# Eighty elementwise operations of the MLPs and of the dilated v projection, taken from VectorE to GpSimd

## The chip, the cores and the metric

The kernel runs on one core of a Trainium2 chip. The metric is device time in microseconds (us) of one execution. TensorE is called PE below, VectorE DVE, ScalarE ACT, GpSimd POOL and SyncE SP, as in the profile.

## The reference

Two layers of an encoder trunk on one sequence of 1024 tokens with 1024 channels. Each layer has a token mixer (layer 0: latent attention with 16 heads; layer 1: three groups of dilated windowed attention) and a squared-ReLU MLP with 4096 hidden channels. Each half normalises its input, shifts and scales it by numbers that come from a conditioning vector (`mods`), and adds its result, times a gate, to the residual. All is float32.

```
for i in range(DEPTH):
    h = rms_norm(x, g) * (1 + scale) + shift
    x = x + gate * mixer(h)          # i=0: mla, i=1: dilated
    h = rms_norm(x, g) * (1 + scale) + shift
    x = x + gate * (square(relu(h @ mlp_w1[i])) @ mlp_w2[i])
```

The v projection of the dilated mixer is, for each of its three groups, a product of h (1024 by 1024) with a weight of 1024 by 1024.

## The kernel before, in words

A float32 product is made of three products in a form that PE takes in one pass: each operand is split into a high part (ACT copies it, L121) and a low part (DVE subtracts the high part from the operand, L122), and `mm3` (L425 to L427) multiplies high with high, low with high, high with low. So every tile of a weight or an activation that reaches PE has one ACT operation and one DVE operation ahead of it: in the MLP the tiles are `dh` and `dl` (made of `ufr`, `w2r`, `w2T`, `w2s`), in the v projection `wvh` and `wvl` (weights, made of `wvr`), `hT`, `hsh` and `hsl` (activations, made of `hk` and of the sums `s`).

The MLP (`mlp7`) and the v projection (`dil_v`) both replace eight block products by seven, in the manner of Strassen and Winograd: quarters of the operands are first added and subtracted, seven products are made, and their results are put together when PSUM is read out.

`mlp7` has an up phase, whose results (`ua`, `ub`, `us`) are stored to DRAM by POOL, and a down phase of seven products with eight steps each. A step is 24 matmuls of 128x512. Step by step the operands are loaded three steps ahead (`d_load`: `ufr` are the stored activations, `w2r` the weights) and formed one step ahead (`d_form`). Of the weights' quarters, product 0 (R11) loads quarters 11 and 12, splits 11 and at once subtracts 11 from 12; that difference and 11 are kept (16 tiles). Product 1 (T2) loads quarter 22, subtracts the kept difference (`w2T`, kept as well), splits that, and at once subtracts the kept 11 from it, in place; this is what product 5 (T3) uses. Product 2 (T1) uses the kept difference, and product 6 (T4) loads quarter 21, subtracts `w2T` (giving `w2s`) and splits the result. When a product is complete, `evict` reads PSUM; in products 3, 4 and 5 it ends with `fin`: z = z times the gate, x = x + z, on tiles of 128x512, and a store of x. The eviction of product 5 runs `fin` twice for each of four tiles (16 operations) and lies in the steps of product 6. In layer 0 those steps also hold the start of the next layer: the first half of its normalised input is transposed on PE (`pst`), shifted on ACT (`hk`) and split (`hT`), and the first weights of the v projection are split (`wvh`, `wvl`).

`dil_v` has 21 products of 48 matmuls, seven for each group, numbered n below. `sums` makes the weight sums of a group, eight subtractions of 128x1024: two in the first product of the group, four in the second, two in the third. The helper `sub` pins them to the order of the program. `h_sums` makes the sums of the activations (`s`, `hk`) on DVE. `out` evicts to a tile `vz` and has POOL store it. All through these stages DVE also adds the conditioning of later layers (`adacc`, L176), 128x1024 at a time.

A scheduler that works before the run puts the instructions of each engine in an order; on the chip each engine runs its own in that order and waits on semaphores.

Of the kernel before, what the change touches and what calls it, by code (L numbers as in the profile page):

```python
# [15 lines left out]
ALU = mybir.AluOpType  # L16
# [25 lines left out]
class K:  # L42
# [1045 lines left out]
    def mlp7(self, l, early, R, steps, xd, out, more=(), nxt=None, keep=None):  # L1088
# [7 lines left out]
        nc, a = self.nc, self.a  # L1096
        NP = FF // 256
        tt = lambda o, x, y, op=ALU.add: nc.vector.tensor_tensor(o, x, y, op=op)
# [6 lines left out]
        with self.tc.tile_pool(name="psM", bufs=8, space=PSUM, reuse_waits="tile") as psp:  # L1105
# [71 lines left out]
            kept = {}  # L1177
# [9 lines left out]
            def d_form(i, g, ld):  # L1187
                rn = order2[i][1]
                u, q = ld
                r = []  # L1190

                def split(x):
                    r.extend(self.X("d" + k, (P, 2, 512)) for k in "hl")
                    self.split(*r[-2:], x)

                split(u)
                if rn == "R11":
                    split(q["11"])
                    tt(q["12"], q["12"], q["11"], ALU.subtract)
                    kept[("T1", g)], kept[("T3", g)] = q["12"], q["11"]  # L1200
                elif rn == "T2":
                    kept[(rn, g)] = w = self.G("w2T", (P, 2, 512), F32)
                    tt(w, q["22"], kept[("T1", g)], ALU.subtract)
                    split(w)
                    tt(kept[("T3", g)], w, kept[("T3", g)], ALU.subtract)
                elif rn == "T4":
                    w = self.X("w2s", (P, 2, 512), F32)
                    tt(w, q["21"], kept[("T2", g)], ALU.subtract)
                    split(w)
                else:  # L1210
                    split(q[rn[1:]] if rn[0] == "R" else kept[(rn, g)])
                return r
# [16 lines left out]
            at = {ci: n for n, ci in enumerate(seq)}  # L1229
# [22 lines left out]
            def d_first(k, made):  # L1252
                if made:
                    fm[k] = d_form(*dsteps[k], ld.pop(k))
                else:
                    ld[k] = d_load(*dsteps[k])
# [37 lines left out]
            at = lambda q, t: q[t // 2][:, t % 2, :]  # L1294
            xs = [None] * 8
            last = len(dsteps) - 1
            c1, c2 = slice(0, 512), slice(512, 1024)
            V, done = {}, []

            def fin(t, c, y):  # L1300

                z = self.T("z")
                tt(z, y, g[:, c], ALU.mult)
                tt(xs[t][:, c], xs[t][:, c], z)

            def evict(i, t, ps):

                add = lambda o, v: tt(o, ps, at(V[v], t))
                new = {0: "S1", 1: "U2", 2: "U4", 5: "U3"}.get(i)
                if new and t == 0:  # L1310
                    V[new] = quad("d" + new)
                if i == 0:
                    nc.scalar.activation(at(V["S1"], t), ps, AF.Copy)
                    return
                if new:
                    add(at(V[new], t), {1: "S1", 2: "U2", 5: "U2"}[i])
                if i > 2:
                    z = self.T("z")
                    add(z, {3: "S1", 4: "U4", 5: "U4"}[i])
                    r, c = {3: (t, c1), 4: (t, c2), 5: (t + 4, c2)}[i]  # L1320
                    fin(r, c, z)
                    out(r, c, xs[r], nc.gpsimd)
                if i == 5:
                    fin(t + 4, c1, at(V["U3"], t))

            more = list(more)
            h = None
            for n, (i, gr) in enumerate(dsteps):
# [4 lines left out]
                for k in {0: (), last - 2: (last - 1, last), last - 1: (), last: ()}.get(n, (n + 1,)):  # L1333
                    fm[k] = d_form(*dsteps[k], ld.pop(k))
                if done:
                    evict(*done.pop(0))
                if gr == 0:
                    ps = [M() for _ in range(4)]
                if i in (3, 5) and gr < 4:
                    t = i * 2 - 6 + gr  # L1340
                    xs[t] = self.load(xd[t * P : (t + 1) * P, :], (P, 1024), "x")
                if (i, gr) == (3, 4):
                    g = self.gate(l, 1)
# [7 lines left out]
                for t in range(4):  # L1351
                    if n == last:
                        down(ps[t], fm[n - 1], t, False, False)
                    down(ps[t], fm[n], t, gr == 0, gr == NP // 2 - 1)
                    if n == last:
                        fin(t + 4, c1, ps[t])
                        out(t + 4, c1, xs[t + 4], nc.sync)
# [232 lines left out]
    def dil_v(self, xs, mods, at0, keep, w11, f11, vd):  # L1590
# [2 lines left out]

        nc, a = self.nc, self.a
        tt = lambda o, x, y, op=ALU.add: nc.vector.tensor_tensor(o, x, y, op=op)
        sub = lambda o, x, y: self.pinned(tt(o, x, y, ALU.subtract))

        prod = [("L11", "R11"), ("L12", "R21"), ("S2", "T2"), ("S1", "T1"), ("S3", "T3"), ("L22", "T4"), ("S4", "R22")]
        seq = [(g, i) for g in range(3) for i in range(7)]
# [5 lines left out]
        V = {}  # L1605
# [94 lines left out]
        with self.tc.tile_pool(name="psV", bufs=8, space=PSUM, reuse_waits="tile") as psp:  # L1700
# [5 lines left out]
            for n, (g, i) in enumerate(seq):  # L1706
# [21 lines left out]
                elif 1 < n < 6:  # L1728
                    x = ("S1", "S3", "L22", "S4")[n - 2]
                    h_form(x, A.pop(1) if x == "L22" else S.pop(x), self.G if x == "L22" else self.X)  # L1730
                ps = [psp.tile([P, 512], F32, tag="m", name=self.nm("psv")) for _ in range(4)]
                l, f = L[prod[i][0]], F.pop(n)
# [13 lines left out]
                if n == last - 2:  # L1746
                    raws = [self.load(hd[k], (P, 2, 512), "h21r", alloc=self.X) for k in range(2)]
                    w = self.dil_weights(0, 0, self.X)
                elif n == last - 1:
# [6 lines left out]
                    w = w()  # L1756
# [606 lines left out]
```

## Time and profile before

| | |
|---|---|
| median of 3 runs | 3253.53 us (3252.06 to 3259.48) |
| profiled execution | 3253.06 us, of which the span of the trace is 3251.3 us |
| mean granted clock of PE | 0.986 |
| PE busy | 96% |
| DVE busy | 74% |
| ACT busy | 53% |
| POOL busy | 28% |

PE is nearly always busy, so what can be gained is the time for which it waits, and what can be lost is time for which it is made to wait. A row of a timeline gives the start, the time taken, the engine, the line, the operation and the tiles, and in brackets the idle time of the engine before it with what ended that. A row of the table by stretches gives the busy time of PE, of the weight loads, of DVE, ACT and POOL in a stretch of the span, then the clock that PE was granted, and the share of the DMA engines. Where a row has "x4" after its tiles, it stands for four instructions in a row.

### The profile page before, as it was taken

What the parts mean: (1) busy time and instruction counts of PE and PEld (TensorE: products, weight loads), DVE (VectorE), ACT (ScalarE), POOL (GpSimd) and SP (SyncE); (2) the same over time, 40 slices, a digit from 0 to 9 for tenths busy, and PEclk for the clock granted to TensorE, in tenths of its full rate; (3) what the DMA queues carried; (4) which work ended last, traced back from release to release, by engine and by line L of the source; (5) the groups of instructions that cost most, each with busy time, mean ns of one, the idle gap of its engine ahead of it and who ended that gap; (6) DMA issues with size and microseconds to landing.
All of it is one profiled execution on the core that took longest, in us unless ns stands there. A gap on an engine that the chain in (4) does not pass through costs nothing. (4 is left out here: it accounts for less than half of the span.)

```text
span 3251.3 us, 50784 instructions
## 1 busy us (share of the span) xinstructions
PE 3134.1 (96%) x18034; PEld 2648.6 (81%) x18034; DVE 2391.6 (74%) x4244; ACT 1735.2 (53%) x3507; POOL 920.1 (28%) x1225
## 2 busy tenths in 40 slices
PE   6989999999999999899999989998999999999999
PEld 6877677778888788778899989997998788888887
DVE  5677777746987876688757877777788588778566
ACT  5547787754544433542236776666655264544342
POOL 7465555520111000001124434444454001110010
PEclk8999999999999999999999999998999999999999
DMA  5352322252555789545648777887777635448564
GB/s 191 120 188 84 103 95 82 66 178 98 206 179 169 276 227 310 162 136 181 220 127 185 177 170 170 187 183 162 171 167 179 192 105 201 160 143 322 196 195 128
DMA packets 538991, 552.32 MB, mean 170 GB/s; under 512 B 199493, under 2 KB 421106, under 8 KB 538730
## 3 DMA queue, kind: packets, MB, share of 16 engines
q1 hardware_dynamic: 484042, 434.61, 47.2%
q0 software_dynamic: 27360, 91.31, 7.5%
q10 hardware_dynamic: 27328, 23.07, 2.6%
q8 instruction: 144, 2.36, 0.3%
q14 instruction: 117, 0.96, 0.1%
HBM read 376.17 MB, written 132.62 MB: 156 GB/s over the span
## 5 line engine op out<-in xcount | busy, mean ns | idle before, releaser
L426 PE MATMUL psm<-dl,dh 128*128 128x512 f32 x896 | 351.2, 392 | 8.6 <-DVE dl L122 8.5
L425 PE MATMUL psm<-hf,wf 128*128 128x512 f32 x896 | 349.5, 390 | 2.6 <-ACT wf L121 2.6
L427 PE MATMUL psm<-dh,dl 128*128 128x512 f32 x896 | 350.0, 391 | 0.0
L426 PE MATMUL psm<-hf,wf 128*128 128x512 f32 x896 | 348.6, 389 | 0.0
L427 PE MATMUL psm<-hf,wf 128*128 128x512 f32 x896 | 346.6, 389 | 0.4 <-DVE wf L122 0.4
L425 PE MATMUL psm<-dh,dh 128*128 128x512 f32 x896 | 334.9, 391 | 4.4 <-ACT dh L121 4.4
L425 PE MATMUL psproj<-wqkh,hTp 128*128 128x256 f32 x1024 | 303.9, 297 | 0.0
L426 PE MATMUL psproj<-wqkl,hTp 128*128 128x256 f32 x1024 | 291.8, 285 | 0.0
L427 PE MATMUL psproj<-wqkh,hTp 128*128 128x256 f32 x1024 | 291.6, 285 | 0.0
L121 ACT ACTIVATE dh<-ufr 128x1024 fp32r<-128x1024 f32 x112 | 118.4, 1057 | 176.3 <-PE psm L427 51.3
L426 PEld LDWEIGHTS psm<-dl,dh 128*128 128x128 f32 x896 | 169.0, 189 | 46.7 <-DVE dl L122 11.8
L425 PEld LDWEIGHTS psproj<-wqkh,hTp 128*128 128x128 f32 x1024 | 198.3, 194 | 9.0 <-issue 0.9
L425 PEld LDWEIGHTS psm<-dh,dh 128*128 128x128 f32 x896 | 168.1, 188 | 41.8 <-ACT dh L121 6.9
L425 PEld LDWEIGHTS psm<-hf,wf 128*128 128x128 f32 x896 | 168.2, 188 | 40.0 <-ACT wf L121 5.5
L426 PEld LDWEIGHTS psproj<-wqkl,hTp 128*128 128x128 f32 x1024 | 198.6, 194 | 0.0
L427 PEld LDWEIGHTS psproj<-wqkh,hTp 128*128 128x128 f32 x1024 | 198.2, 194 | 0.0
L427 PEld LDWEIGHTS psm<-hf,wf 128*128 128x128 f32 x896 | 168.2, 188 | 36.2 <-DVE wf L122 1.1
L427 PEld LDWEIGHTS psm<-dh,dl 128*128 128x128 f32 x896 | 169.2, 189 | 35.0
L426 PEld LDWEIGHTS psm<-hf,wf 128*128 128x128 f32 x896 | 168.2, 188 | 34.3
L122 DVE TENSOR_TENSOR dl<-ufr,dh 128x1024 fp32r<-128x1024 f32 x112 | 136.6, 1220 | 78.3 <-ACT dh L121 59.5
L1846 POOL TENSOR_TENSOR qn<-qn,dgain 128x256 f32<-128x256 f32 x96 | 89.9, 936 | 337.8 <-DVE qn L1844 265.4
L756 DVE TENSOR_REDUCE mx<-pmx 128x1 f32<-128x512 f32 x256 | 164.9, 681 | 27.6 <-PE pmx L754 27.4
(400 smaller groups left out, 8986.1 us busy)
## 6 DMA issues: line engine op xcount, KB each, us to landing
ufr<-uf SPq DMA_DIRECT2D x112, 512.0 KB
adaw<-in_ada_w SPq DMA_DIRECT2D x96, 512.0 KB
w2r<-in_mlp_w SPq DMA_DIRECT2D x96, 512.0 KB
w1r<-in_mlp_w SPq DMA_DIRECT2D x64, 512.0 KB
bt<-bias SPq DMA_DIRECT2D x128, 256.0 KB
qkv<-st SPq DMA_DIRECT2D x32, 512.0 KB
hraw<-qkv SPq DMA_DIRECT2D x32, 512.0 KB
uf<-ub POOLq DMA_DIRECT2D x32, 512.0 KB, 3.8
```

Of the source, the lines that this page charges most:

```text
L121: nc.scalar.activation(hi, src, AF.Copy)
L122: (lo_eng or nc.vector).tensor_tensor(lo, src, hi.bitcast(F32), op=ALU.subtract)
L425: mm(out, lh, rh, start=first, stop=False)
L426: mm(out, lh, rl, start=False, stop=False)
L427: mm(out, ll, rh, start=False, stop=last)
L756: nc.vector.tensor_reduce(maxes[h][:, 2 * j + b : 2 * j + b + 1], ps, op=ALU.max, axis=AX.X)
L1846: nc.gpsimd.tensor_tensor(qq, qq, gain[:, g : g + 1, :].unsqueeze(1).broadcast_to([P, 2, 2, 64]), op=ALU.mult)
```

## The change

Eighty operations go from DVE (`nc.vector`) to POOL (`nc.gpsimd`): in both layers the difference 12 minus 11 (8 each) and the one that is kept for T3 (8 each), 32 of 128x1024; in layer 1 alone the 8 `w2s` of product 6; in layer 0 alone the `fin` of product 5, 16 of 128x512; and in `dil_v` all 24 sums of 128x1024, still pinned, and so pinned among POOL's stores. Line numbers after the change are higher by 1 to 2 (`w2s` is then L1209, `fin` L1304 and L1305, `sub` L1598).

```diff
                 if rn == "R11":
                     split(q["11"])
-                    tt(q["12"], q["12"], q["11"], ALU.subtract)
+                    nc.gpsimd.tensor_tensor(q["12"], q["12"], q["11"], op=ALU.subtract)
                     kept[("T1", g)], kept[("T3", g)] = q["12"], q["11"]
                 elif rn == "T2":
                     kept[(rn, g)] = w = self.G("w2T", (P, 2, 512), F32)
                     tt(w, q["22"], kept[("T1", g)], ALU.subtract)
                     split(w)
-                    tt(kept[("T3", g)], w, kept[("T3", g)], ALU.subtract)
+                    nc.gpsimd.tensor_tensor(kept[("T3", g)], w, kept[("T3", g)], op=ALU.subtract)
                 elif rn == "T4":
                     w = self.X("w2s", (P, 2, 512), F32)
-                    tt(w, q["21"], kept[("T2", g)], ALU.subtract)
+                    eng = nc.gpsimd if l else nc.vector
+                    eng.tensor_tensor(w, q["21"], kept[("T2", g)], op=ALU.subtract)
...
-            def fin(t, c, y):
+            def fin(t, c, y, eng=nc.vector):
                 z = self.T("z")
-                tt(z, y, g[:, c], ALU.mult)
-                tt(xs[t][:, c], xs[t][:, c], z)
+                eng.tensor_tensor(z, y, g[:, c], op=ALU.mult)
+                eng.tensor_tensor(xs[t][:, c], xs[t][:, c], z, op=ALU.add)
...
-                    fin(r, c, z)
+                    eng = nc.gpsimd if i == 5 and l == 0 else nc.vector
+                    fin(r, c, z, eng)
                     out(r, c, xs[r], nc.gpsimd)
                 if i == 5:
-                    fin(t + 4, c1, at(V["U3"], t))
+                    fin(t + 4, c1, at(V["U3"], t), eng)
...
-        sub = lambda o, x, y: self.pinned(tt(o, x, y, ALU.subtract))
+        sub = lambda o, x, y: self.pinned(nc.gpsimd.tensor_tensor(o, x, y, op=ALU.subtract))
```

The first place is the start of product 6 in layer 0. DVE before, from the low part of step 1's weights (`dl_18643`) past that of step 2's (`dl_18708`); the rows with `x` and `z` are `fin`:

```order
L122 TENSOR_TENSOR dl_18643<-w2s_18640,dh_18642 128x1024
L1098 TENSOR_TENSOR x_18394<-x_18394,z_18770 128x512
L122 TENSOR_TENSOR dl_18702<-ufr_18594,dh_18701 128x1024
L1098 TENSOR_TENSOR w2s_18705<-w2r_18596,w2T_17031 128x1024
L1098 TENSOR_TENSOR x_18394<-x_18394,z_18774 128x512
L1098 TENSOR_TENSOR z_18833<-z_18831,gate_17831 128x512
L1098 TENSOR_TENSOR z_18837<-dU_3802_18647,gate_17831 128x512
L122 TENSOR_TENSOR hT_3880_18987<-hk_18988,hT_3879_18986 128x512 x2
L122 TENSOR_TENSOR dl_18708<-w2s_18705,dh_18707 128x1024
```

The same stretch of DVE in the changed kernel, and the part of POOL's queue that belongs to it (before, POOL had only the stores to `xd` there):

```order
L122 TENSOR_TENSOR dl_18643<-w2s_18640,dh_18642 128x1024
L1098 TENSOR_TENSOR z_18831<-psm_18307,dU_3612_17658 128x512
L122 TENSOR_TENSOR dl_18702<-ufr_18594,dh_18701 128x1024
L1209 TENSOR_TENSOR w2s_18705<-w2r_18596,w2T_17031 128x1024
L122 TENSOR_TENSOR hT_3861_18892<-hk_18893,hT_3860_18891 128x512 x2
L122 TENSOR_TENSOR wvl_18922<-wvr_18812,wvh_18921 128x1024
L122 TENSOR_TENSOR wvl_18926<-wvr_18814,wvh_18925 128x1024
L122 TENSOR_TENSOR dl_18708<-w2s_18705,dh_18707 128x1024
```

```order
L1304 TENSOR_TENSOR z_18770<-z_18768,gate_17831 128x512
L1305 TENSOR_TENSOR x_18351<-x_18351,z_18718 128x512
L2279 DMA xd<-x_18351 128x512
L1304 TENSOR_TENSOR z_18774<-dU_3802_18647,gate_17831 128x512
L1305 TENSOR_TENSOR x_18394<-x_18394,z_18770 128x512
L1304 TENSOR_TENSOR z_18833<-z_18831,gate_17831 128x512
L1305 TENSOR_TENSOR x_18394<-x_18394,z_18774 128x512
L2279 DMA xd<-x_18394 128x512
L1304 TENSOR_TENSOR z_18837<-dU_3802_18647,gate_17831 128x512
```

The `fin` rows have left DVE, and two `hT` and two `wvl`, which stood ahead of `dl_18643` before, now stand between it and `dl_18708`. From `w2s_18602` of step 0 on, DVE of the changed kernel has ten operations of 128x1024 and six of 128x512 with two SBUF inputs up to and with `dl_18708`, and six that read PSUM; POOL has the 16 of `fin`.

The second place is the second product of the last group of `dil_v`. DVE before; `wvl_20403` is the low part of the sum `wvr_20320`, and it is what the third product begins with:

```order
L1595 TENSOR_TENSOR wvr_20226<-wvr_20320,wvr_20226 128x1024
L176 SCALAR_TENSOR_TENSOR adacc_20306<-adaw_20462,cond,adacc_20306 128x1024
L228 SCALAR_TENSOR_TENSOR mod_20301<-mod_20301,colc 128x8
L1595 TENSOR_TENSOR wvr_20320<-wvr_20320,wvr_20142 128x1024
L1595 TENSOR_TENSOR wvr_20228<-wvr_20322,wvr_20228 128x1024
L176 SCALAR_TENSOR_TENSOR adacc_20306<-adaw_20465,cond,adacc_20306 128x1024
L1595 TENSOR_TENSOR wvr_20322<-wvr_20322,wvr_20144 128x1024
L122 TENSOR_TENSOR wvl_20403<-wvr_20320,wvh_20402 128x1024
```

DVE and POOL of the changed kernel there:

```order
L176 SCALAR_TENSOR_TENSOR adacc_20306<-adaw_20389,cond,adacc_20306 128x1024
L122 TENSOR_TENSOR wvl_20331<-wvr_20224,wvh_20330 128x1024
L225 TENSOR_TENSOR mod_20301<-psac_20292,colc 128x8
L176 SCALAR_TENSOR_TENSOR adacc_20306<-adaw_20462,cond,adacc_20306 128x1024
L228 SCALAR_TENSOR_TENSOR mod_20301<-mod_20301,colc 128x8
L176 SCALAR_TENSOR_TENSOR adacc_20306<-adaw_20465,cond,adacc_20306 128x1024
L176 SCALAR_TENSOR_TENSOR adacc_20306<-adaw_20542,cond,adacc_20306 128x1024
L176 SCALAR_TENSOR_TENSOR adacc_20306<-adaw_20545,cond,adacc_20306 128x1024
L122 TENSOR_TENSOR wvl_20403<-wvr_20320,wvh_20402 128x1024
```

```order
L1639 DMA v<-vz_20317 128x512
L1598 TENSOR_TENSOR wvr_20142<-wvr_20226,wvr_20142 128x1024
L1598 TENSOR_TENSOR wvr_20144<-wvr_20228,wvr_20144 128x1024
L1598 TENSOR_TENSOR wvr_20226<-wvr_20320,wvr_20226 128x1024
L1598 TENSOR_TENSOR wvr_20320<-wvr_20320,wvr_20142 128x1024
L1598 TENSOR_TENSOR wvr_20228<-wvr_20322,wvr_20228 128x1024
L1598 TENSOR_TENSOR wvr_20322<-wvr_20322,wvr_20144 128x1024
```

The six sums now form a chain on POOL behind the four stores of the product before, and DVE has five `adacc` between the last store of the product before and `wvl_20403`; two of them stood behind it.

## The prediction

> **What bounds the kernel now.** I read the page first, then what PE waits for, then PE's waits in time in the five stages that the change touches. The page's first row says that PE sets the time; DVE is the next engine, and POOL has room on average.
>
> ```profile
> PE 3134.1 (96%) x18034; PEld 2648.6 (81%) x18034; DVE 2391.6 (74%) x4244; ACT 1735.2 (53%) x3507; POOL 920.1 (28%) x1225
> ```
>
> An average says nothing about a stage, so next come the waits of PE (total, times, longest) on tiles that DVE's queue feeds in the MLPs and in the v projection.
>
> ```profile
> PE psm L426 <- DVE dl L122: 8.5, 4, 4.1
> PE psm L425 <- ACT dh L121: 4.4, 3, 3.2
> PE psv L425 <- ACT wvh L121: 2.4, 1, 2.4
> PE psv L425 <- ACT hsh L121: 2.0, 1, 2.0
> PE psv L426 <- DVE wvl L122: 2.0, 2, 1.1
> ```
>
> They add up to 19.3 us. That, with some time at a lower clock behind each wait, is all that a shorter DVE queue could bring. By stretches (PE busy stands first, then weight loads, DVE, ACT, POOL, and the granted clock):
>
> ```profile
> 1076.00:1095.00 19.00, 16.05 (x70) 12.89 (x70) 11.57 (x14) 7.06 (x10) 1.30 (x2) 0.98 1.03 377
> 1360.00:1395.00 35.00, 26.43 (x117) 20.08 (x117) 33.87 (x45) 19.02 (x24) 2.16 (x4) 0.90 0.54 184
> 1420.00:1480.00 60.00, 53.62 (x236) 43.18 (x235) 55.29 (x63) 30.05 (x38) 3.25 (x6) 0.91 0.24 80
> 1594.00:1612.00 18.00, 18.00 (x82) 14.88 (x80) 17.90 (x19) 5.46 (x7) 0.54 (x1) 1.00 0.63 205
> 2965.00:3010.00 45.00, 45.00 (x200) 37.24 (x200) 43.17 (x39) 20.23 (x22) 0.00 (x0) 1.00 0.74 246
> ```
>
> PE loses 8.6 us at the start of layer 0's product 6 (1360 to 1395) and 6.4 us in group 0 of `dil_v` (1420 to 1480), and DVE is over 90% busy in both. It is as full in the last two stretches, where PE waits for nothing: these stages can only lose.
>
> **What an operation costs on either engine, and what it blocks.** By shape (count, then busy time and mean ns):
>
> ```profile
> L1098 DVE TENSOR_TENSOR w2r<-w2r,w2r 128x1024 f32<-128x1024 f32 x16 | 19.4, 1221 | 11.1 <-DMA w2r<-in_mlp_w 11.1
> L122 POOL TENSOR_TENSOR pl<-p,ph 128x1024 fp32r<-128x1024 f32 x58 | 141.4, 2438 | 136.1 <-ACT ph L121 125.9 <-DVE mod L225 5.1 <-PE pav L883 4.6
> L1937 POOL TENSOR_TENSOR ph<-pd,ph 128x512 f16<-128x512 f32 x62 | 74.1, 1195 | 59.3 <-ACT ph L1936 55.6 <-issue 3.7
> L122 POOL TENSOR_TENSOR oT<-O,oT 128x512 fp32r<-128x512 f32 x16 | 25.2, 1596 | 11.5 <-ACT oT L121 11.5
> L122 DVE TENSOR_TENSOR pl<-p,ph 128x1024 fp32r<-128x1024 f32 x70 | 94.0, 1344 | 72.5 <-ACT ph L121 65.6 <-issue 3.9 <-POOL pl L122 2.2
> L1860 DVE TENSOR_TENSOR kT<-psq,kT 128x512 fp32r<-128x512 f32 x96 | 65.9, 686 | 36.0 <-ACT kT L1859 35.7
> ```
>
> In a queue a wide operation (128x1024) takes 1.135 us of DVE's time (two that overlap a little take 2.35, in part 4) and a narrow one 0.60 (two take 1.28, in part 2); on POOL I take 2.40 and 1.20, by the rows of 2438 and 1195 ns. The same `pl` takes DVE 1344 ns in the mean, where POOL works beside it, against 1221 for `w2r`. One place shows why:
>
> ```profile
> 287.37 3.50 POOL L924 TENSOR_TENSOR O<-ot,rl 64x512 f32<-64x512 f32 x2
> 287.45 2.29 DVE L122 TENSOR_TENSOR pl<-p,ph 128x1024 fp32r<-128x1024 f32 x1 [0.19 <-POOL pl L122]
> ```
>
> DVE's `pl` begins 0.08 us behind the first of POOL's two and takes 2.29 us instead of 1.22, as if it stood still for POOL's operation; it then works while POOL's second one, in turn, stands. `kT`, with one operand in PSUM, keeps to 686 ns. So I count: a DVE operation with two SBUF inputs and a POOL operation exclude each other and take turns. Then an operation that is moved takes 1.135 us out of DVE's queue and puts up to 2.40 in (narrow: 0.60 and 1.20): a gain where DVE has pauses, PSUM work, or nothing urgent; a loss of 1.27 each where it is full.
>
> The Trainium skill, "SBUF — State Buffer", section "Who interferes with whom", states this as a rule: DVE with two SBUF inputs and a GpSimd instruction that reads SBUF exclude each other for a whole instruction. It speaks against most of this change, and the rows agree (2.29 for 1.22); without it, each move would be worth its 1.135 us wherever DVE is late.
>
> **1. The differences, layer 0, products 0 and 1.** DVE stands still for 4.42 us behind a load that only the moved operation needs, and PE waits for the `dl` behind it:
>
> ```profile
> 1091.24 1.23 DVE L1098 TENSOR_TENSOR w2r<-w2r,w2r 128x1024 f32<-128x1024 f32 x1 [4.42 <-DMA w2r<-in_mlp_w]
> 1093.66 0.50 PE L426 MATMUL psm<-dl,dh 128*128 128x512 f32 x1 [2.95 <-DVE dl L122]
> 1112.91 1.06 ACT L121 ACTIVATE dh<-ufr 128x1024 fp32r<-128x1024 f32 x1 [6.52 <-DMA ufr<-uf]
> 1113.88 1.04 ACT L121 ACTIVATE dh<-w2r 128x1024 fp32r<-128x1024 f32 x1
> 1116.24 0.62 PE L425 MATMUL psm<-dh,dh 128*128 128x512 f32 x2
> ```
>
> That wait goes, with some 1.7 us at a lower clock after it. But the next limit is a load: `dh` of step 4 waits for `ufr`, is ready at 1114.92, and is used at 1116.24. The DMA share is full (1.03), so the load comes no earlier, PE arrives 4.7 us sooner and waits 3.4 there, with a slow start of its own. Net -0.5 (bounds -1.5 and +1). Product 1 of layer 0 has none of PE's waits above, and fewer `adacc` beside it than its counterpart in layer 1 (part 5): 0 (up to +1).
>
> **2. `fin` at the end of layer 0.**
>
> ```profile
> 1360.31 1.22 DVE L1098 TENSOR_TENSOR w2s<-w2r,w2T 128x1024 f32<-128x1024 f32 x1
> 1376.28 1.21 PE L425 MATMUL psm<-dh,dh 128*128 128x512 f32 x4 [3.24 <-ACT dh L121]
> 1381.61 0.80 PE L426 MATMUL psm<-dl,dh 128*128 128x512 f32 x1 [4.11 <-DVE dl L122]
> 1386.15 1.28 DVE L122 TENSOR_TENSOR hT<-hk,hT 128x512 fp32r<-128x512 f32 x2
> 1387.36 1.21 DVE L122 TENSOR_TENSOR dl<-w2s,dh 128x1024 fp32r<-128x1024 f32 x1
> 1387.64 1.07 PE L425 MATMUL psm<-dh,dh 128*128 128x512 f32 x4
> ```
>
> The `dl` of step 2 (`dl_18708`) is done at 1388.57, and PE takes it at once. In the new order DVE has ten wide and six narrow operations from `w2s_18602` to it, and 15 of POOL's 16 come between, one by one. 1360.31 + 10 x 1.135 + 6 x 0.60 + 15 x 1.20 = 1393.3; the PSUM reads lie beside POOL's. That is 4.7 later. By the same count step 1's `dl` comes some 1.5 sooner, which only lengthens PE's wait for step 2. After the wait of 4.11, the 20 matmuls to 1387.64 took 6.0 us, where 0.227 each makes 4.5 (four take 1.07 in the last row, the last of them 0.39, as one does in part 4, so three starts take 0.68): a slow start of 1.5 follows such a wait, and here a longer one comes. Sum +6.2, and +0.3 for the sums of group 0, which then run beside the later steps. +6.5 (bounds +4 and +9).
>
> **3. The sums of group 0.**
>
> ```profile
> 1448.36 1.24 PE L425 MATMUL psv<-wvh,hsh 128*128 128x512 f32 x4 [2.04 <-ACT hsh L121]
> ...
> 1455.17 2.08 PE L425 MATMUL psv<-wvh,hsh 128*128 128x512 f32 x4 [2.37 <-ACT wvh L121]
> 1463.82 0.50 PE L426 MATMUL psv<-wvl,hsh 128*128 128x512 f32 x1 [0.83 <-DVE wvl L122]
> ```
>
> These are the first, third and last of four waits, together 6.38 us, which is all of the 60 - 53.62 of the table; at a clock of 0.91 the rest was some 4 us slower. DVE has eight sums of 1.135 here. In the changed kernel six of them run on POOL while the MLP ends; three of these stood in DVE's queue between the transposed input and the `hk` that `hsh` is made of, so `hsh` comes 3.4 us sooner, more than its wait of 2.04, and what is behind it gains more still. -9.8 (bounds -10.6 and -5: the last two sums on POOL meet `hsl` on DVE).
>
> **4. The sums of groups 1 and 2.**
>
> ```profile
> 1594.45 2.35 DVE L1595 TENSOR_TENSOR wvr<-wvr,wvr 128x1024 f32<-128x1024 f32 x2
> 1606.13 1.21 DVE L122 TENSOR_TENSOR wvl<-wvr,wvh 128x1024 fp32r<-128x1024 f32 x1
> 1613.13 0.39 PE L426 MATMUL psv<-wvl,hsh 128*128 128x512 f32 x1
> ```
>
> In group 2 PE takes `wvl_20403` at 1613.13; it was ready at 1607.34. With six sums of 2.40 in turn with five `adacc` and one `wvl`, all as wide as the sums, it starts at 1594.45 + 14.4 + 6 x 1.135 = 1615.7 and ends at 1616.9: PE waits 3.8, and 1.5 of slow start follow, +5.3. Were DVE's six first and only the four sums that it needs ahead of it, it ends near 1613.4: +0.3. In group 1 two `adacc` lie beside, and 5 us are left: 0 (up to +1).
>
> **5. Layer 1.** In product 1 DVE is full: five operations for a step of 24 matmuls, 5.7 us for 5.44.
>
> ```profile
> 2977.00 1.23 DVE L122 TENSOR_TENSOR dl<-w2T,dh 128x1024 fp32r<-128x1024 f32 x1 [1.71 <-ACT dh L121]
> 3012.09 1.22 DVE L122 TENSOR_TENSOR dl<-w2T,dh 128x1024 fp32r<-128x1024 f32 x1
> 3019.68 0.39 PE L426 MATMUL psm<-dl,dh 128*128 128x512 f32 x1
> ```
>
> Eight moves at +1.27 make 10.2; the pause of 1.71 takes some, and the last `dl` had 19.68 - 13.32 = 6.4 in hand: +2 (bounds 0 and +5). Product 0 holds one of the four waits for `dl` above and, as in layer 0, a load that lands only just in time behind it: 0. In product 6 nothing waits now, and the eight `w2s` come from an idle POOL: +0.3 (up to +1).
>
> **The sum** for the likeliest case: -0.5 + 6.5 - 9.8 + 5.3 + 2 + 0.3 = +3.8. Against the profiled execution's own 3253.06 that is 3256.9, so **3257**; the median of the runs is 0.5 above that execution. About 0.2% (6.5 us) is what a measurement can tell from no change, so this counts as the same. Its own range is 3247 to 3259.5.
>
> **The rivals.** *Faster, 3240*: DVE's pauses and PSUM reads take up more of POOL's time than I grant, so that terms 4 and 5 go, term 2 becomes -0.9 (step 1's `dl` sooner, step 2's hardly later), and 1 and 3 bring their full 1.5 and 10.6: -13. For it: POOL was idle there, and waits disappear in three places. Against it: DVE's 33.87 us of 35. *Slower, 3263*: the narrow operations in product 6. At 1.20 they cost +4.7; the other narrow POOL row above has 1.60, and 15 x 0.40 adds 6, to 3263. It decides from about 1.38 on (15 x 0.18 = 2.7 brings the sum to +6.5). *The change does nothing where it acts*, because loads set those stages as in product 0: terms 1 and 3 near zero. Group 0's table row, with a DMA share of 0.24, speaks against it; then only the costs of 2, 4 and 5 are left, +14.1, 3267.
>
> **Chances.** Forecast 0.42, faster 0.25, slower by `fin` 0.26, no gain 0.07; that gives faster 0.25, same 0.42, slower 0.33. The range takes in the first rival's value and the last's: 3240 to 3268, the outermost sums of the bounds being rarer than 2 in 10.
>
> **What would show it.** The wait for `hsh` at 1448 gone, and PE's slow stretch with it (term 3). A wait of 6 us for the `dl` of product 6's step 2, with `w2s` and `dl` on DVE at twice their 1.22 us (term 2). A new wait of some 4 us at the third product of group 2 (term 4). DVE operations of 2 to 3.6 us in layer 1's product 1 (term 5). If DVE keeps to 1.22 beside POOL, the exclusion is wrong, and the time falls below 3240.

## The result, and the profile after

The changed kernel is slower: 3270.82 us in the median of 6 runs (3266.15 to 3276.2), against 3253.55 of 6 runs before; ratio 1.0052, 95% interval 1.004 to 1.0065, so +17 us (+13 to +21). A second series of 5 runs gave 3264.63 us, ratio 1.0041 (1.0028 to 1.0054), +13 us (+9 to +18). The forecast was 3257 and "the same", its range to 3268.

The profiled execution after took 3266.15 us, 13.1 more than the one before. The page's first row: POOL has 224 us more, and DVE, which was relieved of 80 operations, has 33 us more as well.

```profile
PE 3140.7 (96%) x18034; PEld 2652.9 (81%) x18034; DVE 2424.3 (74%) x4164; ACT 1731.5 (53%) x3507; POOL 1144.4 (35%) x1305
```

A DVE operation that waits for POOL counts as busy, so "busy" hides the loss on DVE. PE's waits show it (after; total, times, longest): `dl` had 8.5 and `dh` 4.4 before; the four waits of group 0 (6.4 us) are gone but for one of 0.8, and a new one for `wvl`, in group 2, has come.

```profile
PE psm L426 <- DVE dl L122: 18.3, 10, 5.6
PE psm L425 <- ACT dh L121: 6.9, 4, 5.2
PE psv L426 <- DVE wvl L122: 2.5, 1, 2.5
```

By stretches after (the same columns as before; the stretches are those of before, shifted to where the same work now lies, and lengthened where it takes longer):

```profile
1365.00:1402.00 37.00, 24.24 (x97) 18.64 (x97) 34.56 (x26) 16.33 (x22) 28.77 (x20) 0.80 0.50 167
1433.00:1484.00 51.00, 50.15 (x236) 41.30 (x235) 48.15 (x52) 29.43 (x38) 18.92 (x10) 1.00 0.23 83
1599.00:1625.00 26.00, 23.50 (x98) 19.06 (x97) 25.89 (x16) 6.41 (x8) 21.30 (x11) 0.93 0.50 170
2971.00:3024.00 53.00, 50.08 (x219) 40.46 (x218) 51.60 (x31) 18.60 (x21) 26.63 (x8) 1.00 0.60 208
```

Group 0 of `dil_v` makes the same 236 matmuls in 51 us instead of 60, at full clock. Around `fin` PE is idle for 12.8 of 37 us and at a clock of 0.80; in the two stretches where it waited for nothing before, it now loses 2.5 and 2.9.

To place the difference, the start of each matmul was subtracted from that of the same matmul before, and the median taken around the ends of the stages. The table has the growth of that difference in each stage, in us, in both profiled executions of the changed kernel, beside the forecast's terms:

| stage | forecast | first | second |
|---|---|---|---|
| layer 0, product 0 | -0.5 | +1.2 | +2.3 |
| layer 0, product 1 | 0 | +2.2 | +2.1 |
| `fin` (layer 0, product 6) | +6.5 | +7.8 | +8.2 |
| `dil_v`, group 0 | -9.8 | -8.9 | -8.8 |
| `dil_v`, group 2 | +5.3 | +4.2 | +4.3 |
| layer 1, product 0 | 0 | -0.2 | -0.2 |
| layer 1, product 1 | +2 | +3.9 | +3.9 |
| layer 1, product 6, to the end of the span | +0.3 | +3.3 | +3.3 |
| sum | +3.8 | +13.5 | +15.1 |

In the last row PE's matmuls come 4.5 us later in both executions; 1.1 of it comes back behind the last matmul, which was followed by 6.6 us of other work before and is followed by 5.4 after.

The untouched stages differ by several us between executions (ahead of layer 0's MLP by -0.1 to +5 in the executions of this study, in the dilated attention by -6 to +3), which is why one execution's span says little about effects of this size, and the table by stages much.

The waits behind those rows, PE after, in the order of the table (products 0 and 1 and `fin` of layer 0, group 2, and products 1 and 6 of layer 1; of `fin` and of layer 1's product 1 the longest alone):

```profile
1108.08 0.80 PE L426 MATMUL psm<-dl,dh 128*128 128x512 f32 x1 [3.94 <-DVE dl L122]
...
1165.31 0.50 PE L426 MATMUL psm<-dl,dh 128*128 128x512 f32 x1 [1.48 <-DVE dl L122]
...
1382.33 2.07 PE L425 MATMUL psm<-dh,dh 128*128 128x512 f32 x4 [5.24 <-ACT dh L121]
...
1399.88 0.80 PE L426 MATMUL psm<-dl,dh 128*128 128x512 f32 x1 [5.61 <-DVE dl L122]
...
1619.92 0.80 PE L426 MATMUL psv<-wvl,hsh 128*128 128x512 f32 x1 [2.50 <-DVE wvl L122]
...
3017.11 0.50 PE L426 MATMUL psm<-dl,dh 128*128 128x512 f32 x1 [1.16 <-DVE dl L122]
...
3236.15 0.50 PE L426 MATMUL psm<-dl,dh 128*128 128x512 f32 x1 [2.56 <-DVE dl L122]
```

All but the last stand behind DVE operations that a POOL operation held: for `dh` it is the `w2s` that ACT waits for, and at 1165.31 a load stands between. At the last, DVE's `dl` takes its usual 1.21 us and waits for ACT's `dh` of a `w2s` that is made on POOL itself. DVE after, at the places of product 0, product 1 and `fin`, of layer 1's product 1 and of its product 6 (before, `us` took 0.69 us):

```profile
1098.58 2.89 DVE L1098 TENSOR_TENSOR us<-ua 128x512 f32<-128x512 f32 x1 [0.23 <-ACT ua L1140]
1103.98 2.91 DVE L1098 TENSOR_TENSOR us<-ub,us 128x512 f32<-128x512 f32 x1
...
1154.63 3.41 DVE L122 TENSOR_TENSOR dl<-w2T,dh 128x1024 fp32r<-128x1024 f32 x1
...
1162.89 1.23 DVE L1098 TENSOR_TENSOR w2T<-w2r,w2r 128x1024 f32<-128x1024 f32 x1 [2.59 <-DMA w2r<-in_mlp_w]
...
1373.33 0.69 DVE L1098 TENSOR_TENSOR z<-psm,dU 128x512 f32<-128x512 f32 x1 [2.44 <-POOL z L1304]
...
1390.34 6.07 DVE L122 TENSOR_TENSOR hT<-hk,hT 128x512 fp32r<-128x512 f32 x2
...
3004.43 1.23 DVE L122 TENSOR_TENSOR dl<-ufr,dh 128x1024 fp32r<-128x1024 f32 x1
3005.57 3.42 DVE L176 SCALAR_TENSOR_TENSOR adacc<-adaw,cond,adacc 128x1024 f32<-128x1024 f32 x1
...
3234.88 1.21 DVE L122 TENSOR_TENSOR dl<-w2s,dh 128x1024 fp32r<-128x1024 f32 x1
```

And POOL after, beside them:

```profile
1098.52 2.41 POOL L1199 TENSOR_TENSOR w2r<-w2r,w2r 128x1024 f32<-128x1024 f32 x1 [2.30 <-DMA w2r<-in_mlp_w]
...
1103.97 2.36 POOL L1199 TENSOR_TENSOR w2r<-w2r,w2r 128x1024 f32<-128x1024 f32 x1
...
1141.90 15.06 POOL L1205 TENSOR_TENSOR w2r<-w2T,w2r 128x1024 f32<-128x1024 f32 x3 [2.08 <-DVE w2T L1098]
...
1393.36 2.49 POOL L1305 TENSOR_TENSOR x<-x,z 128x512 f32<-128x512 f32 x2
...
3004.48 3.43 POOL L1205 TENSOR_TENSOR w2r<-w2T,w2r 128x1024 f32<-128x1024 f32 x1 [3.50 <-DVE w2T L1098]
...
3231.21 2.59 POOL L1209 TENSOR_TENSOR w2s<-w2r,w2T 128x1024 f32<-128x1024 f32 x1
```

`adacc` took 1.28 us where POOL is idle and takes 3.42 beside a subtraction on POOL that itself takes 3.43: POOL stands while DVE's `dl` runs to 3005.66, then DVE's `adacc` stands until POOL ends at 3007.91. The three end at 3008.99, which is about what they would take one behind the other.

### The profile page after: what moved, and what is told of

Read it like the earlier page. It is cut to its first block, busy times and chain, and to the rows that moved or that the text cites. A ratio compares the mean times of both kernels' runs of the same rounds, so it can differ in the third digit from the quotient of the medians.

```text
span 3264.4 us, 50887 instructions
## 1 busy us (share of the span) xinstructions
PE 3140.7 (96%) x18034; PEld 2652.9 (81%) x18034; DVE 2424.3 (74%) x4164; ACT 1731.5 (53%) x3507; POOL 1144.4 (35%) x1305
## 3 DMA queue, kind: packets, MB, share of 16 engines
q8 instruction: 144, 2.36, 0.3%
## 5 line engine op out<-in xcount | busy, mean ns | idle before, releaser
L122 DVE TENSOR_TENSOR dl<-ufr,dh 128x1024 fp32r<-128x1024 f32 x112 | 157.1, 1403 | 75.7 <-ACT dh L121 57.1
L122 POOL TENSOR_TENSOR pl<-p,ph 128x1024 fp32r<-128x1024 f32 x58 | 141.3, 2436 | 138.3 <-ACT ph L121 128.0
```

What stands on the lines that cost most here:

```text
L122: (lo_eng or nc.vector).tensor_tensor(lo, src, hi.bitcast(F32), op=ALU.subtract)
```

## The experiments

**Each part alone.** Theory A: DVE's operations with two SBUF inputs and POOL's exclude each other, and so every moved operation costs DVE more than it frees. Theory B: the loss comes from the parts together or from the new order of instructions. Four kernels have one part of the diff each: `fin`, the line of `sub`, the two lines of the differences for T1 and T3, and the line of `w2s`.

```diff
+                    eng = nc.gpsimd if i == 5 and l == 0 else nc.vector      # only_fin
+        sub = lambda o, x, y: self.pinned(nc.gpsimd.tensor_tensor(...))      # only_sums
+                    nc.gpsimd.tensor_tensor(q["12"], ...); T3 likewise        # only_diffs
+                    eng = nc.gpsimd if l else nc.vector                       # only_w2s
```

> The kernel before with one part of the change, the 16 operations of fin in layer 0, on GpSimd. Theory A (a VectorE operation with two SBUF inputs and a GpSimd operation exclude each other, so each move delays VectorE): the low part of step 2 of product 6 comes late as in the changed kernel, and nothing else changes: +6 to +8 us against the kernel before. Theory B (the loss of the changed kernel comes from the parts acting together, or from the new order of instructions): 0 to +2 us. If the move only shortens VectorE's queue: -4 to -8 us.

> The kernel before with the 24 sums of dil_v alone on GpSimd. Theory A: group 0 gains 8 to 10 us, group 2 loses 4 to 5 at its third product, together -6 to -4 us, and both stretches look as in the changed kernel. Theory B: the loss in group 2 is not there without the other parts, -9 us. If the sums were a loss by themselves: 0 or above.

> The kernel before with the 32 differences 12 minus 11 and those for T3 alone on GpSimd. Theory A: +1 in product 0 and +2 in product 1 of layer 0, 0 and +4 in layer 1, together +5 to +9 us, from VectorE operations of 2 to 3.5 us beside GpSimd's. Theory B: within 2 us of the kernel before.

> The kernel before with the 8 differences w2s of product 6 in layer 1 alone on GpSimd. Theory A: +3 to +5 us, in the last steps of product 6, where w2s stands behind stores of GpSimd that wait for VectorE, and then excludes VectorE. Theory B: within 1 us. The four parts together, if they add up, should make the loss of the changed kernel: +13 to +17 us.

Measured, by ratio: `fin` 1.0023 (1.0013 to 1.0034), +7.5 us; the sums 0.9992 (0.9983 to 1.0001), -2.6 us, not clear of zero, where -6 to -4 was expected; the differences 1.0022 (1.0013 to 1.003), +7.2 us; `w2s` 1.0008 (0.9997 to 1.0018), +2.6 us, not clear of zero by itself and below the +3 to +5 expected. Together +14.7 us, which is inside the intervals of both series of the whole change. By stages `fin` lost 8.1 at the end of layer 0 and no more after it; the sums lost 2.4 beside the last steps of layer 0, gained 10.5 in group 0 and lost 3.1 in group 2; the differences lost 2.7 and 2.1 in products 0 and 1 of layer 0 and 3.9 in product 1 of layer 1 (and 2.4 more at a wait in product 3 of layer 0, which the kernel with group 0's sums alone, further below, lengthens by as much, though no part of the change lies near it); `w2s` lost 2.9 to the end of the span. The waits for `fin` and for the sums are the ones of the whole change. PE in the kernel with `fin` alone:

```profile
1394.94 0.80 PE L426 MATMUL psm<-dl,dh 128*128 128x512 f32 x1 [5.31 <-DVE dl L122]
```

PE in the kernel with the sums alone:

```profile
1612.21 0.50 PE L426 MATMUL psv<-wvl,hsh 128*128 128x512 f32 x1 [2.81 <-DVE wvl L122]
```

Theory B falls as far as it needs the parts together; each loss is there with its part alone. Its other form, the new order of instructions, is left to the next experiment.

**Work on POOL that nobody waits for.** DVE keeps all its work. POOL, ScalarE, or POOL with one input instead of two, does additional work at the places of the T3 differences (each kernel has one of the three lines). In the two kernels with the work on POOL, PE's and DVE's operations keep the order of the kernel before:

```diff
                     tt(kept[("T3", g)], w, kept[("T3", g)], ALU.subtract)
+                    for k in range(2):
+                        nc.gpsimd.tensor_tensor(self.T("dup"), w[:, k], kept[("T1", g)][:, k], op=ALU.subtract)  # dup_pool
+                        nc.scalar.activation(self.T("dup"), w[:, k], AF.Copy)                                    # dup_act
+                        nc.gpsimd.tensor_scalar(self.T("dup"), w[:, k], 2.0, None, op0=ALU.mult)                 # dup_one
```

> The kernel before, and beside each difference for T3, which stays on VectorE, GpSimd makes two subtractions of 128x512 into a scratch tile that nobody reads (32 in all, in product 1 of both layers). The order of every other engine is that of the kernel before, instruction for instruction. Theory A (exclusion): 16 times about 1.2 us go into VectorE's queue in layer 1, 19 us, of which 8 are covered (6.4 in hand and a pause of 1.7): +9 to +11 us there, and +2 to +5 in layer 0. Theory B (what costs time is that something waits for a slower operation or stands behind it in GpSimd's queue, or the new order): nothing waits for these, so within 1 us.

> The same, but the scratch tiles are written by ScalarE (32 copies of 128x512 from the same tile). ScalarE is about 45% busy there. Theory A: VectorE keeps its 1.22 us, and the time is that of the kernel before within 2 us. If any further reader of these tiles slowed VectorE down, this one would cost as much as GpSimd's.

> As dup_pool, but GpSimd's 32 extra operations have one SBUF input (the tile times 2, 128x512) instead of two. The order of the other engines is that of the kernel before. If every GpSimd operation that reads SBUF excludes VectorE's operations with two SBUF inputs: VectorE's operations beside it take 2 us or more and the loss is about 10 us times the ratio of the durations, +4 to +12. If only two inputs on both sides collide: within 2 us of the kernel before.

Two inputs on POOL: 1.0046 (1.0029 to 1.0063), +15 us (+9 to +20). By stages it is +9.9 in layer 1's product 1, as theory A expected, and nothing in layer 0's, where +2 to +5 was expected. In layer 0 it was POOL that stood, and not DVE:

```profile
1147.13 23.56 POOL L1207 TENSOR_TENSOR dup<-w2T,w2r 128x512 f32<-128x512 f32 x1 [10.67 <-DVE oh L1426]
```

The third of the 16, it came to its turn only when DVE paused for 0.13 us at 1169.55, and by then DVE had formed nearly all of product 1; the other thirteen ran behind it. Why POOL stood there and DVE in layer 1 is open. DVE by shape in layer 1's product 1 of this kernel (before, all of these take 1220 ns in the mean, and `adacc` 1280):

```profile
L122 DVE TENSOR_TENSOR dl<-ufr,dh 128x1024 fp32r<-128x1024 f32 x11 | 18.9, 1715 | 1.8 <-ACT dh L121 1.8
L1098 DVE TENSOR_TENSOR w2r<-w2T,w2r 128x1024 f32<-128x1024 f32 x7 | 13.9, 1996 | 0.0
...
L122 DVE TENSOR_TENSOR dl<-w2T,dh 128x1024 fp32r<-128x1024 f32 x7 | 10.7, 1525 | 0.0
L176 DVE SCALAR_TENSOR_TENSOR adacc<-adaw,cond,adacc 128x1024 f32<-128x1024 f32 x5 | 9.5, 1890 | 0.0
```

So 16 operations that no instruction of another engine waits for cost 10 us there. This shows the exclusion as a cause by itself, without a new order of instructions. ScalarE's copies cost nothing (0.9996, 0.9987 to 1.0005), though the order of instructions moved a little in that kernel; DVE's `dl` keeps its time:

```profile
L122 DVE TENSOR_TENSOR dl<-ufr,dh 128x1024 fp32r<-128x1024 f32 x13 | 15.8, 1219 | 0.2 <-ACT dh L121 0.2
```

With one input on POOL nothing is lost either: 0.9999 (0.999 to 1.0008). The collision is there but smaller. A `dl` beside such an operation takes 1.63 us, where beside POOL's two-input ones of the same size it took 2.31. POOL with one input (all of layer 1, then one in layer 0 with DVE idle beside it), then DVE of the same kernel:

```profile
L1207 POOL TENSOR_SCALAR dup<-w2T 128x512 f32<-128x512 f32 x16 | 30.4, 1917 | 28.9 <-DVE w2T L1098 28.9
...
1177.19 1.49 POOL L1207 TENSOR_SCALAR dup<-w2T 128x512 f32<-128x512 f32 x1
```

```profile
2992.65 1.63 DVE L122 TENSOR_TENSOR dl<-ufr,dh 128x1024 fp32r<-128x1024 f32 x1
2994.20 1.63 DVE L122 TENSOR_TENSOR dl<-w2T,dh 128x1024 fp32r<-128x1024 f32 x1
```

16 times 0.41 are 6.6 us at most, and the stage had 6.4 in hand and a pause of 1.7, so the time alone could not show this collision.

**Half of `fin`.** The first two of the four tiles go to POOL, the others stay on DVE.

```diff
+                    eng = nc.gpsimd if i == 5 and l == 0 and t < 2 else nc.vector
```

> As only_fin, but only the first two of the four tiles of fin in layer 0 are on GpSimd (8 operations). Theory A (each operation adds its time to VectorE's queue): about half of only_fin's 8 us at the end of layer 0, +3 to +5. If the loss comes from the last operations alone (the transposed tiles and weights that moved between the low parts of step 1 and 2), it goes: -2 to +1.

Measured 1.0007 (0.9998 to 1.0016), +2.3 us, and by stages +3.9 at the end of layer 0, against 8.1 for all of it: half of the operations, about half of the cost. PE in this kernel waits for `dh` and for the `dl` of step 2, as with all of `fin`, and shorter for step 2 (3.67 against 5.31):

```profile
1378.79 2.07 PE L425 MATMUL psm<-dh,dh 128*128 128x512 f32 x4 [5.90 <-ACT dh L121]
1391.67 0.79 PE L426 MATMUL psm<-dl,dh 128*128 128x512 f32 x1 [3.67 <-DVE dl L122]
```

**Is it POOL's queue in product 6 of layer 1?** There `w2s` stands in POOL's queue behind stores of x that wait for DVE. This kernel has `w2s` on POOL and issues those stores from SyncE.

```diff
-                    out(r, c, xs[r], nc.gpsimd)
+                    out(r, c, xs[r], nc.sync if l else nc.gpsimd)
```

> As only_w2s (the 8 w2s of product 6 in layer 1 on GpSimd), but the stores of x behind fin in layer 1 are issued by SyncE, so that w2s no longer stands in GpSimd's queue behind stores that wait for VectorE. If the 2.4 to 4 us that only_w2s lost in the last steps come from that queue, they vanish: 0 to +1 us. If they come from the exclusion of VectorE alone, they stay: +2 to +4.

Measured 1.0006 (0.9997 to 1.0014), +2.0 us, and +4.8 by stages from product 6 to the end of the span, where `w2s` alone had +2.9. The loss stays without the queue; the long wait lies at another step, and here it is for a `dl` that POOL's next `w2s` held. PE in this kernel, DVE and POOL:

```profile
3219.52 0.80 PE L426 MATMUL psm<-dl,dh 128*128 128x512 f32 x1 [2.74 <-DVE dl L122]
...
3216.09 3.37 DVE L122 TENSOR_TENSOR dl<-w2s,dh 128x1024 fp32r<-128x1024 f32 x1
...
3215.73 2.66 POOL L1208 TENSOR_TENSOR w2s<-w2r,w2T 128x1024 f32<-128x1024 f32 x1 [3.05 <-PE psm L426]
```

**What is worth keeping.** Only group 0's sums are in a stage that gains. Two kernels keep them on POOL, the second with one more move: of the differences, only the one behind which DVE stood still for 4.42 us.

```diff
+        sub = lambda g, o, x, y: self.pinned((nc.vector if g else nc.gpsimd).tensor_tensor(o, x, y, op=ALU.subtract))  # both
+                    (nc.gpsimd if (l, g) == (0, 2) else nc.vector).tensor_tensor(q["12"], ...)                         # best
```

> The kernel before with the 8 sums of group 0 of dil_v alone on GpSimd, those of groups 1 and 2 on VectorE. Theory A: the loss at the third product of group 2 goes, the gain of group 0 (about 10 us) stays, less the 2 us that its sums cost beside the last steps of layer 0: -9 to -6 us against the kernel before. Theory B: no better than only_sums (-3).

> The sums of group 0 on GpSimd as in sums_g0, and of the differences 12 minus 11 only the one on GpSimd behind which VectorE stood still for 4.42 us (layer 0, group 2 of 8). In the prediction the wait that this takes away was to come back at a load one step later: then product 0 of layer 0 gains 0 to 1.5 us. If instead the other differences on GpSimd made the loss there, and no load, it gains 3 to 4.7. The whole: -11 to -6 us against the kernel before.

Group 0's sums alone: 0.9979 (0.9969 to 0.9988), 3247.25 us in the median of 10 runs, -7 us: faster than both kernels. By stages it loses 1.6 beside layer 0's last steps and gains 8.9 in group 0. This stretch of that kernel, where before PE was busy for 53.62 of 60 us at a clock of 0.91:

```profile
1425.00:1485.00 60.00, 59.14 (x276) 48.69 (x275) 57.15 (x63) 31.54 (x40) 18.38 (x10) 1.00 0.34 118
```

With the one difference as well it is 0.9983 (0.9974 to 0.9992), not better, and short of the -11 to -6 us expected. PE is 4.4 us ahead behind the wait that is gone, and by the end of product 0 all of that, and 0.6 more, has been given back, at a load. PE, then ACT, of that kernel:

```profile
1116.24 1.20 PE L425 MATMUL psm<-dh,dh 128*128 128x512 f32 x4 [2.44 <-ACT dh L121]
```

```profile
1114.19 1.06 ACT L121 ACTIVATE dh<-ufr 128x1024 fp32r<-128x1024 f32 x1 [10.63 <-DMA ufr<-uf]
```

**The changed kernel again.**

> The changed kernel once more, for a ratio with a smaller interval and a second profile. If the four parts add up (their ratios make +15 us): +13 to +17 us. The 4.7 us by which its profiled execution was below its median would then lie in stages that the change does not touch.

Its ratio and its stages stand above. It is within the +13 to +17 expected of parts that add up; the first series' median is 6 us above the second's, and its 4.7 above its own profiled execution can't be placed, since only one execution of a series is traced.

## Why the prediction was wrong

The mechanism was right in each stage in which it was priced. What failed is the price in five of the six stages that lose: three terms were put near nothing (products 0 and 1 of layer 0, product 6 of layer 1) and measured +1.2 to +3.3 each, and two were mis-sized (`fin`, product 1 of layer 1). The predicted +3.8 became +13.5 to +15.

- **Exclusion.** As forecast, shown by work that nobody waits for. What the forecast did not have is that it is partial where POOL's operation has one SBUF input. The Trainium skill, "SBUF — State Buffer", section "Who interferes with whom", has DVE with two SBUF inputs and any GpSimd instruction that reads SBUF exclude each other for the whole instruction. The two-input rows agree (3.42 and 3.43 us for 1.28 and about 2.4); the one-input rows do not fully: `dl` takes 1.63 for 1.22, though POOL's operation takes 1.49 by itself.
- **Part 1, product 0: -0.5, measured +1.2 and +2.3.** The step that the wait goes and comes back at a load held: the kernel with that one difference moved shows both. What failed is that the other seven subtractions were taken as free. Two of them (2.41 us from 1098.52, 2.36 from 1103.97) each met a `us` on DVE, a sum of the up phase's results, which took 2.89 and 2.91 us instead of 0.69. PE waits 3.94 for the `dl` behind these before it comes to the load, and is then too late to wait there.
- **Part 1, product 1: 0, measured +2.1.** I looked at PE's waits before, found none, and took that for reserve. Three T3 differences took 15.06 us on POOL; the first took 8.4, of which it stood for some 6 while DVE worked on, and then the three took turns with DVE and made three of its operations late by 2.2 each. A load that waits for the DVE operation behind them is issued only at 1159.20, DVE stands 2.59 for it up to 1162.89, and PE 1.48 behind that. An average reserve does not cover a bunch.
- **Part 2: +6.5, measured +7.8 and +8.2.** The wait for step 2 came, 5.61 for the 6 expected, with `hT` rather than `dl` held longest. What was off is the size of one POOL operation: free of DVE these narrow ones take 1.25 us (two in 2.49) to 1.30, not 1.20, and 15 times 0.05 to 0.1 is 0.8 to 1.5. One wait that the count did not have, DVE's 2.44 for a `z` of POOL's, falls in time in which POOL worked, so the sum of turns holds. Half of the operations cost about half. The rival that named 1.38 as the point from which this alone decides did not come true.
- **Part 3: -9.8, measured -8.9.** Right; the waits at 1448 to 1464 are gone. The cost beside layer 0's last steps, 0.3 in the sum, was 1.6 to 2.4 in the two kernels with sums and without `fin`.
- **Part 4: +5.3, measured +4.2.** Right; the wait was 2.50 instead of 3.8, with the slow start behind it as forecast.
- **Part 5, product 1: +2, measured +3.9.** Right in kind. The reserve of 6.4 us was the last step's; three waits (0.79, 1.16 and 0.97) came one step after another, where less was in hand, with `adacc` at 3.42.
- **Part 5, product 6: +0.3, measured +3.3.** The step that failed most. "Nothing waits now, and `w2s` come from an idle POOL" looked at the two engines' pauses, and not at what each of the eight would hold: DVE has the `fin` of this layer there, and its operations took up to 2.9 us. The count of part 2 should have been made here too. In the longest wait of the changed kernel it is POOL's own `w2s` that comes late, behind two stores; without these the loss is no smaller, as the kernel with stores on SyncE shows, and comes from a `dl` of 3.37 us. How much of the loss is exclusion, and how much is that POOL takes 2.4 us for a `w2s` that PE is waiting for, was not separated.

The differences between the columns of the table add up to 10 us in the first and 11 in the second execution, and with the +3.8 they make +13.5 and +15.1, inside the intervals of both series. The range's upper end was set by single rivals; that five of the costs were low together, and by one cause in the main, was not among them.

## What to carry to other kernels

Before an elementwise operation with two SBUF inputs goes from VectorE to GpSimd, count what stands in VectorE's queue beside it: where such a pair met in this kernel it took the sum of both times, so a move costs VectorE up to GpSimd's 2.4 us for the 1.135 it frees. Here it paid only where the moved work could run in a stretch before the engine became tight, as group 0's sums did (-7 us), and it cost even where nothing waited before, because a few held operations in a row use up what a step has in hand. Work with one SBUF input on GpSimd, or copies on ScalarE, cost nothing in the one place where they were tried.

## What the runs showed of the hardware that I had not expected

- Turns are not strict. Mostly the engines alternate (3.42 and 3.43), but two `hT` took 6.07 us while POOL made three narrow operations in a row behind a store that it issued. The other way round, the first of the three POOL subtractions in 15.06 us stood for some 6 us while DVE's operations passed, and in the kernel with scratch work one took 23.56 us, until DVE paused for 0.13. No run here shows what decides whose turn it is.
- A narrow one-input operation on POOL holds a wide DVE operation up by 0.41 us, a two-input one by 1.1 (2.31 for 1.22).
- After every wait of over 3.2 us for a `dl` PE goes on at 0.427 us for each matmul of 128x512 instead of 0.227, for six to thirteen of them; around the wait of 5.61 the granted clock was 0.50 from 1398 to 1404. The Trainium skill, "TensorE: Matmul & The Clock Gate", section "Part 1: The HAM clock gate (the "warmup" mystery)", has the same figure (426.7 ns) for a half-rate clock, which it lets follow an idle window of about 3.4 us. Here shorter waits can bring it too: one of 2.50 did (after, 1619.92), and one of 2.81 at the same place in the kernel with the sums alone did not. Where it comes, it adds 1 to 3 us to what the wait shows, by an estimate of 0.2 for each slow matmul.
